# A two-layer decoder trunk in float32: W1 units between the seven-product pairs of the pass before

## The chip, the cores and the metric

The kernel runs on one core of a Trainium2 chip. The metric is the device time of one execution in microseconds; the figures are medians of several runs. TensorE is PE in the profile (its weight loads PEld), VectorE DVE, ScalarE ACT, GpSimd POOL, and SyncE, which here only issues transfers, SP.

## What is computed

The input is 256 positions of 2048 float32 values. Layer 0 is a gated short convolution and an MLP, layer 1 is attention (MLA) and an MLP; after each of the four sub-layers stands a layer norm of the scaled sum. The change lies in the two MLPs, which are the largest part: each multiplies 256 x 2048 by 2048 x 8192 and that by 8192 x 2048.

```python
def sq_relu_mlp(x, w1, w2):
    return jnp.square(jax.nn.relu(x @ w1)) @ w2

for layer in range(DEPTH):            # DEPTH = 2
    mix = short_conv_mixer(...) if layer < N_A else mla_mixer(...)
    h = layer_norm(ALPHA * h + mix, ln_g[layer, 0], ln_b[layer, 0])
    h = layer_norm(ALPHA * h + sq_relu_mlp(h, mlp_w1[layer], mlp_w2[layer]),
                   ln_g[layer, 1], ln_b[layer, 1])
return h
```

## The kernel before

**Split numbers.** Every float32 operand is held as two float32r parts: `hi`, a cast on ScalarE (line 127), and `lo`, the difference on VectorE (line 128). A product is then hi by hi, hi by lo and lo by hi, the sum taken in PSUM. The weights come raw from HBM, are split on the chip and used once.

**The stream of weights.** `stream` lists every weight tile in the order of use. `take(n, look)` hands over the next n and, before that, prepares what comes after them, up to `look` pieces ahead: a tile of W1 or a plain tile of W2 is one piece (one transfer of 512 KB, one `hi`, one `lo`), a pair for seven products is three (two transfers; `hi` and `lo` of three tiles of 1024 columns and one of 512, and the combinations that they are made of, lines 162 to 170). `RAW` tiles hold raw weights, `WA` pairs of tiles hold split ones. The transfers are issued on SP's queue.

**An MLP.** `mlp` goes over the 8192 hidden columns in `NQ` = 8 passes of 1024. A pass has `QC` = 8 units: unit m makes 128 hidden columns for all 256 positions, 32 matmuls on the 16 K tiles of W1 (`mm_run`: at each K tile `high`, 512 columns at line 215, and `low`, 256 columns at line 219). Its sums are put together by `whole` (ScalarE copies a half out of PSUM at line 355, VectorE adds the other at line 356), then relu and square (lines 718, 719) and the split. In the first unit of a pass, `TURNED` swaps `high` and `low` at one K tile.

After its eight units a pass multiplies the 1024 hidden columns by its part of W2. Passes 0 and 7 do it plainly. In the six passes between (`FAST`) two K tiles make a pair, and with two blocks of 128 positions and two blocks of 512 output columns a pair is a 2 x 2 product of blocks. `fast_products` computes that in seven products instead of eight (the Winograd form of Strassen's method; `FACTORS` names each product's two factors). The factors of the activations, the `forms`, are sums of blocks, made by `form` (lines 707 to 710) from two units. The output columns are two groups of 1024. In a pass, group 1 comes first, with three pairs of seven products and one plain pair of eight (`MIXED` = "sssp"; `EVEN` splits one of its matmuls in two), then group 0 with four pairs of seven. The products of three matmuls each are at lines 300, 302 and 303 (`dot`).

**The sums.** Each of the seven products has a PSUM bank and its own running sum over the passes: three in `acc`, four (`OWN`) in `sums`. Before a group starts, ScalarE copies running sums into PSUM (`resumed`, line 612); afterwards it copies them back (`put_back`, line 616), or VectorE adds what was begun from nothing (`keep`, line 624). In the last pass `fold` (line 676) combines the seven sums to four blocks. The residual of the layer norm waits in `xres` in SBUF meanwhile. In the first MLP `begin` (`ln.prepare`, line 415) scales it and takes a mean away before the layer's end; in the second, `extra` (`turn_residual`) turns it with TensorE and adds it to `acc` during passes 1 to 4.

**Order.** The program is written in one order; the instructions of each engine are put in order when the kernel is built, by the written order and by what is ready, and then run strictly in that order.

Of the kernel before, what the change touches and what calls it, by code (L numbers as in the profile page):

```python
# [16 lines left out]
P = 128  # L17
# [16 lines left out]
RAW, WA = 5, 8  # L34
# [3 lines left out]
MIXED = "sssp"  # L38
EVEN = (QC - 1, "22")
# [14 lines left out]
def trunk(ctx: ExitStack, tc: tile.TileContext, xT, vecs, lead, w_first, w_in, w_out, w_kv, w_q, w_uk, w_uv,  # L54
# [27 lines left out]

    def mlp_stream(l):
        out = []
        for q in range(NQ):
            out += halves(w1[l, q * QC:(q + 1) * QC])
            if q not in FAST:
                out += halves(w2[l, q])
                continue
            for j, kind in enumerate(MIXED):  # L90
                out += [(w2f[l, q, 1, j, 0], w2f[l, q, 1, j, 1])] if kind == "s" else \
                    halves(w2[l, q, 2, j]) + halves(w2[l, q, 3, j])
            out += [(w2f[l, q, 0, j, 0], w2f[l, q, 0, j, 1]) for j in range(QC // 2)]
        return out
# [210 lines left out]
    def held(x, t):  # L305

        return [x[:, o + t * P:o + (t + 1) * P] for o in (0, T)]
# [35 lines left out]
    def fast_products(ps, x, forms, j, fresh, ready, onto=()):  # L343

        b, = take(1)
        a = {"11": held(x[2 * j], 0), "12": held(x[2 * j + 1], 0), "22": held(x[2 * j + 1], 1)}
        for i in range(4):
            a[f"S{i + 1}"] = [forms[:, j, o, i * P:(i + 1) * P] for o in range(2)]
        for p, l, r in FACTORS:
            dot(ps[p], b[r], a[l], p in fresh, p in ready, onto=p in onto)  # L350
# [41 lines left out]
    class Norm:  # L392
# [10 lines left out]
        def prepare(self, m, bank=None):  # L403

            d = xres[:, m, :]
# [11 lines left out]
        def count(self, m):  # L417
            d = xres[:, m, :]
# [21 lines left out]
        def wide(self, m):  # L440
            d, x, g = xres[:, m, :], self.xd[m], self.gain(m)[0]
# [31 lines left out]
        def normal(self, m, dst=None):  # L473

            g, b = self.gain(m)
            d = xres[:, m, :]
# [22 lines left out]
    def add(ps, m):  # L499
        d = xres[:, m, :]  # L500
        nc.vector.tensor_tensor(d, d, ps[:, :T], ALU.add)
# [73 lines left out]
    def mlp(idx, ln, blocks, fast, begin=None, extra=None, last=False):  # L575
# [25 lines left out]
        sums = fast.tile([P, 4, 2, BW], F32, name=f"sums{idx}")  # L601

        def place(p, g):

            return sums[:, OWN.index(p), g, :] if p in OWN else \
                block(*{"2": (2 * g, 0), "3": (2 * g + 1, 0), "4": (2 * g, 1), "22": (2 * g + 1, 1)}[p])

        def resumed(p, g, name, bank):

            ps = psum(name, bank)  # L610
            if q != FAST[0] or p not in OWN:
                nc.scalar.copy(ps, place(p, g))
            return ps
# [4 lines left out]
        def keep(p, g, ps):  # L618

            at = place(p, g)  # L620
            if q == FAST[0] and p in OWN:
                nc.scalar.copy(at, ps)
            else:
                nc.vector.tensor_tensor(at, at, ps, ALU.add)

        def resume(busy, free, ps, m):

            b2, b3, b4, b6 = free
            b1, b5, b7, b22 = busy
            for p, bank in {3: (("3", b3),), 4: (("2", b2),), 5: (("4", b4), ("1", b1)), 6: (("6", b6), ("5", b5)),  # L630
                            7: (("7", b7), ("22", b22))}.get(m, ()):
                ps[p] = resumed(p, 1, f"ps_r{p}", bank)

        def down_pairs(h, forms, busy, free, ps):

            b2, b3, b4, b6 = free
            b1, b5, b7, b22 = busy
            new = set(OWN) if q == FAST[0] else set()
            onto = set(ps) - new
            for j, kind in enumerate(MIXED):  # L640
                if kind == "s":
                    last = j == MIXED.rindex("s")
# [545 lines left out]
```

## Time and profile before

| | |
|---|---|
| median of 3 runs | 2000.58 us (2000.33 to 2001.18) |
| span of the profiled execution, first to last instruction | 1994.9 us |
| that execution's own time | not recorded beside its span |
| first fast pass to the end of pass 7, first MLP | from 452.8 to 997.5 us |
| the same, second MLP | from 1394.6 to 1941.8 us |
| granted TensorE clock | 1.000 |
| moved by the DMA queues | 385.85 MB |

A row of the timeline is the start in us, the duration, the engine, the line, and out<-in by the program's names. Matmuls overlap, so what one costs is the time from its start to the next one's start, not its duration. The same holds, to a smaller degree, for VectorE and ScalarE. A row of a group is: line, engine, operation, out<-in, count, busy us, mean ns of one, idle time of the engine before them and what ended it. A row of the windows is: stretch and length in us, then the busy time of each engine with its number of instructions, the granted clock, the DMA engines' share and GB/s.

### The profile page before, as it was taken

To read this page: it belongs to the slowest core of one execution; us is meant where nothing else is said; L and a number is where in the kernel's file an instruction comes from. 1 tells how busy PE (TensorE), PEld (TensorE's weight loads), DVE (VectorE), ACT (ScalarE), POOL (GpSimd) and SP (SyncE) were. 2 spreads that over 40 slices of the span, in tenths; PEclk is the share of its full clock that TensorE was granted. 3 is DMA by queue.
4 is the path that set the end of the run, shared out by engine and by line. 5 is a ranking of instruction groups with operands and counts; after the bars stand their busy time and mean duration, and the time that the engine had idled before them with its cause. 6 is when DMAs were issued, how large, how long until landed. Compare 5 with 4: busy or idle time off the path is not lost.

```text
span 1994.9 us, 30180 instructions
## 1 busy us (share of the span) xinstructions
PE 1987.7 (100%) x11110; PEld 1737.2 (87%) x11110; DVE 1709.4 (86%) x2555; ACT 1354.9 (68%) x2154; POOL 2.3 (0%) x21
## 2 busy tenths in 40 slices
PE   9999999999999999999999999999999999999998
PEld 8888888988888888888889998898888888888886
DVE  8667667797999989989978988777899999999985
ACT  6444445586778778777756755558677787887772
POOL 0000000000000000000000000000000000000000
PEclk9999999999999999999999999999999999999999
DMA  8666666565657466574855543656464656656483
GB/s 318 205 191 187 190 190 190 179 193 157 212 170 251 148 216 221 177 243 147 281 171 159 170 140 123 201 180 195 146 233 155 232 161 220 222 178 233 150 269 130
DMA packets 106853, 385.85 MB, mean 193 GB/s; under 512 B 11857, under 2 KB 12625, under 8 KB 106449
## 3 DMA queue, kind: packets, MB, share of 16 engines
q1 hardware_dynamic: 106560, 383.79, 59.5%
q8 instruction: 87, 1.43, 0.3%
q14 instruction: 62, 0.50, 0.1%
q10 hardware_dynamic: 144, 0.13, 0.0%
HBM read 381.78 MB, written 2.10 MB: 192 GB/s over the span
## 4 chain that ended last, share of the span: by engine, by line
PE 98%; DVE 1%; ACT 1%; issue 0%; DVEq 0%; ACTq 0%
PE ps_u L215 20%; PE ps_l L215 13%; PE ps_u L219 10%; PE ps_l L219 7%; PE ps_f L300 4%; PE ps_f L303 4%; PE ps_f L302 4%; PE ps_r L303 4%; PE ps_r L302 4%; PE ps_r L300 4%; PE ps_d L300 2%; PE ps_d L302 2%; PE ps_d L303 2%; PE ps_w L249 2%; PE ps_w L248 2%; PE ps_w L247 2%
## 5 line engine op out<-in xcount | busy, mean ns | idle before, releaser
L128 DVE TENSOR_TENSOR lo<-raw,hi 128x1024 fp32r<-128x1024 f32 x710 | 861.8, 1220 | 190.6 <-ACT hi L127 119.9
L127 ACT CAST hi<-raw 128x1024 fp32r<-128x1024 f32 x710 | 741.8, 1051 | 247.4 <-PE ps_l L215 98.1
L215 PE MATMUL ps_u<-xhl,hi 128*128 128x512 f32 x1792 | 621.7, 392 | 0.0
L219 PE MATMUL ps_u<-xhl,lo 128*128 128x256 f32 x1792 | 498.2, 279 | 0.0
L215 PEld LDWEIGHTS ps_u<-xhl,hi 128*128 128x128 f32 x1792 | 334.5, 187 | 73.6 <-ACT acc L595 0.2
L219 PEld LDWEIGHTS ps_u<-xhl,lo 128*128 128x128 f32 x1792 | 338.1, 189 | 1.8
L215 PE MATMUL ps_l<-xhl_a,hi 128*128 128x512 f32 x704 | 244.1, 393 | 0.0
L219 PE MATMUL ps_l<-xhl_a,lo 128*128 128x256 f32 x704 | 195.4, 279 | 0.0
L215 PEld LDWEIGHTS ps_l<-xhl_a,hi 128*128 128x128 f32 x704 | 132.1, 188 | 29.9
L219 PEld LDWEIGHTS ps_l<-xhl_a,lo 128*128 128x128 f32 x704 | 131.9, 188 | 0.2
L127 ACT CAST hi_t<-raw_t 128x1024 fp32r<-128x1024 f32 x84 | 88.5, 1054 | 45.8 <-DVE raw_t L162 41.4
L162 DVE TENSOR_TENSOR raw_t<-raw,raw 128x1024 f32<-128x1024 f32 x84 | 102.3, 1218 | 1.8 <-DMA raw<-in_w2f_dram 1.5
L128 DVE TENSOR_TENSOR lo_t<-raw_t,hi_t 128x1024 fp32r<-128x1024 f32 x84 | 102.4, 1219 | 0.2
L718 ACT ACTIVATE fp<-fp 128x256 f32<-128x256 f32 x96 | 40.0, 416 | 63.2 <-DVE fp L356 62.6
L215 PE MATMUL ps_l<-z,hi 128*128 128x512 f32 x240 | 82.4, 391 | 0.0
L300 PE MATMUL ps_d<-hi,h 128*128 128x512 f32 x192 | 75.0, 391 | 0.0
L302 PE MATMUL ps_d<-lo,h 128*128 128x512 f32 x192 | 75.0, 390 | 0.0
L303 PE MATMUL ps_d<-hi,h 128*128 128x512 f32 x192 | 74.8, 389 | 0.0
L249 PE MATMUL ps_w<-xd,hi 128*128 128x258 f32 x256 | 72.7, 284 | 0.0
L248 PE MATMUL ps_w<-xd,lo 128*128 128x258 f32 x256 | 72.3, 282 | 0.0
L247 PE MATMUL ps_w<-xd,hi 128*128 128x258 f32 x256 | 72.3, 282 | 0.0
L215 PE MATMUL ps_l<-oT,hi 128*128 128x512 f32 x208 | 71.3, 391 | 0.0
(296 smaller groups left out, 3963.7 us busy)
## 6 DMA issues: line engine op xcount, KB each, us to landing
raw<-in_w_dram SPq DMA_DIRECT2D x344, 512.0 KB, 4.5
raw<-in_w2f_dram SPq DMA_DIRECT2D x168, 512.0 KB, 3.9
raw<-in_w_in_dram SPq DMA_DIRECT2D x88, 512.0 KB, 4.2
raw<-in_w_out_dram SPq DMA_DIRECT2D x32, 512.0 KB, 3.7
raw<-in_w_o_dram SPq DMA_DIRECT2D x32, 512.0 KB, 4.2
raw<-in_w_kv_dram SPq DMA_DIRECT2D x10, 512.0 KB, 3.7
raw<-in_w_q_dram SPq DMA_DIRECT2D x8, 512.0 KB, 4.0
raw<-in_w_uk_dram SPq DMA_DIRECT2D x8, 512.0 KB, 3.9
```

Of the source, the lines that this page charges most:

```text
L127: nc.scalar.copy(hi, src)
L128: nc.vector.tensor_tensor(lo, src, hi.bitcast(F32), ALU.subtract)
L162: nc.vector.tensor_tensor(t.rearrange(two, a=2), b12.unsqueeze(1).to_broadcast([P, 2, BW]), r1.rearrange(two, a=2), ALU.subtract)
L215: nc.tensor.matmul(ps, w[blk // 8][0][:, blk % 8, :], x, start=first, stop=False)
L219: nc.tensor.matmul(ps[:, :T], w[blk // 8][1][:, blk % 8, :], x[:, :T], start=False, stop=last)
L247: nc.tensor.matmul(ps[:, :W], hi, x[k][:, :W], start=k == 0, stop=False)
L248: nc.tensor.matmul(ps[:, :W], lo, x[k][:, :W], start=False, stop=False)
L249: nc.tensor.matmul(ps[:, :W], hi, x[k][:, W:], start=False, stop=k == NC - 1)
L300: nc.tensor.matmul(ps, x[0], w[0], start=first, stop=False, skip_group_check=onto)
L302: nc.tensor.matmul(ps[:, at], x[0], w[1][:, at], start=False, stop=False, skip_group_check=onto)
L303: nc.tensor.matmul(ps, x[1], w[0], start=False, stop=last, skip_group_check=onto)
L718: nc.scalar.activation(f, f, AF.Relu)
```

## The change

Group by group and pass by pass becomes step by step. A step is one W1 unit of the running pass, followed by one pair of seven products that belongs to units made `SHIFT` = 5 steps and more before: pass 1's units 0 to 4 have no pair beside them, then 48 steps have one, and pass 7's units 5 to 7 have none. All 48 pairs of an MLP use seven products.

- The groups alternate like a snake (pass 1: group 1, then 0; pass 2: 0, then 1), so that a group goes on from one pass into the next. Once in each pass, after the fourth pair, all seven banks are copied out and the other group's seven copied in (`put_back` and `resume`, both ScalarE). `keep` is gone.
- The seven sums and a unit take the eight banks: all units of paired steps use the bank "unit"; units without a pair take turns on "6" and "unit".
- A pair's relu, square, forms and split are made at once over both units in one tile `u` of 8 x 128 columns; the seven left factors lie side by side in `factors` and are split in one go of 7 x 128 columns.
- Every unit that follows a pair has the turned step (`TURN`).
- The ring grows (`RAW` 5 to 7, `WA` 8 to 9), and `take` prepares 7 pieces ahead at a unit and 6 at a pair. `sums` takes the place of the residual in SBUF: in the first MLP the residual is prepared in pass 1, sent to DRAM by five transfers and fetched back by four of 512 KB after pass 7, on GpSimd's queue; in the second, `extra` reads it in the first four units of pass 1.

```diff
-RAW, WA = 5, 8
+RAW, WA = 7, 9
-MIXED = "sssp"
-EVEN = (QC - 1, "22")
+SHIFT = 5
+
+
+def TURN(q, m):
+    return m == 0 or not (q == 1 and m < SHIFT or q == NQ - 1 and m > SHIFT)
...
+    held_x = [xres]
+    parked = ctx.enter_context(tc.tile_pool(name="parked", bufs=1, space=bass.MemoryType.DRAM)).tile(
+        [P, NC, T], F32, tag="parked", name="parked")
...
+    def steps():
+
+        for q in range(1, NQ):
+            for m in range(QC):
+                p, i = (q, m - SHIFT) if m >= SHIFT else (q - 1, m + QC - SHIFT)
+                yield q, m, (p, i // NB, i % NB, (p % 2) ^ (i // NB)) if p in FAST else None
...
+    LEFT = ("11", "22", "12", "S1", "S3", "S2", "S4")
+
+    def fast_products(ps, x, j, fresh, ready, onto=()):
+
+        b, = take(1, 6)
+        a = {n: [x[j // 2][:, j % 2, o, i * P:(i + 1) * P] for o in range(2)] for i, n in enumerate(LEFT)}
         for p, l, r in FACTORS:
             dot(ps[p], b[r], a[l], p in fresh, p in ready, onto=p in onto)
...
+        def form(u):
+
+            a21, a11, a12, s1, s2, s4 = (u[:, i * P:(i + 1) * P] for i in (0, 1, 3, 4, 6, 7))
+            two = u.rearrange("p (i c) -> p i c", c=P)
+            nc.vector.tensor_tensor(s1, a21, u[:, 2 * P:3 * P], ALU.add)
+            nc.vector.tensor_tensor(two[:, 5:7, :], two[:, 0:5:4, :], a11.unsqueeze(1).to_broadcast([P, 2, P]),
+                                    ALU.subtract)
+            nc.vector.tensor_tensor(s4, a12, s2, ALU.subtract)
+
+        def finish_pair(j, u):
+            f = factors[j // 2][:, j % 2]
+            if q in FAST:
+                form(u)
+                split(f[:, 0, :], f[:, 1, :], u[:, P:])
+            else:
+                split(f[:, 0, :2 * T], f[:, 1, :2 * T], u[:, :2 * T])
...
+        base = Banks.count
+        bank = {p: (base + i) % 8 for i, p in enumerate(("6", "unit", "3", "1", "5", "7", "2", "4"))}
+        factors = [act.tile([P, QC // 4, 2, 7 * P], F32R, tag=tag, name=f"h{idx}{tag}") for tag in ("c", "a2")]
...
+        def resume(p, g, at=None):
+
+            ps[p] = psum(f"ps_{p}", bank[at or p])
+            onto.discard(p)
+            if p in OWN and begun[g] == FAST[0]:
+                fresh.add(p)
+            else:
+                nc.scalar.copy(ps[p], place(p, g))
+                onto.add(p)
...
+        def products_of(p, i, j, g):
+
+            nonlocal folds
+            order = [f[0] for f in FACTORS]
+            end = i == 0 or p == FAST[-1]
+            fast_products(ps, factors, j, set(fresh), order if j == NB - 1 and end else (), onto)
+            fresh.clear()
+            if j == NB - 1 and end:
+                begun[g] = 0
+                for o in order:
+                    put_back(o, g, ps[o])
+                    if i == 0:
+                        resume(o, 1 - g)
+            if p == FAST[-1] and j == NB - 1:
+                folds = chain(folds, fold(g))
+
+        for q, m, pair in steps():
+            lone = pair is None
+            if q == FAST[0] and m == SHIFT:
+                for o, _, _ in FACTORS:
+                    resume(o, 1)
+            w = take(2, 7)
+            at = "6" if lone and m % 2 == 0 else "unit"
+            un = psum("ps_u", bank[at])
+            mm_run([(w, un)], xhl, 0, NC, NC, turned=TURNED if TURN(q, m) else None)
+            if m % 2 == 0:
+                u = fast.tile([P, 8 * P], F32, tag="fp", name="fp")
+            whole(un, u[:, (m % 2) * T:(m % 2 + 1) * T])
+            if m % 2:
+                for function in (AF.Relu, AF.Square):
+                    nc.scalar.activation(u[:, :2 * T], u[:, :2 * T], function)
+                if m > 1 or lone:
+                    finish_pair(m // 2, u)
+            if extra and q == FAST[0] and m < NB:
+                for t in range(2):
+                    extra(block, m, t, spare[1 + (2 * m + t) % 3])
+            if begin and q == FAST[0] and m < SHIFT:
+                begin(range(3 * m + 1, 3 * m + 4))
+                nc.gpsimd.dma_start(parked[:, 3 * m + (m > 0):3 * m + 4, :], held_x[0][:, 3 * m + (m > 0):3 * m + 4, :])
+            if q == FAST[0] and m == SHIFT:
+                sums = act.tile([P, 4, 2, BW], F32, tag="xres", name=f"sums{idx}")
+            if q == NQ - 1:
+                for _ in range(3 if m >= SHIFT else 2):
+                    next(folds, None)
+            if pair:
+                products_of(*pair)
+            if m == 1 and not lone:
+                finish_pair(0, u)
...
+        held_x[0] = act.tile([P, NC, T], F32, tag="xres", name="xback")
+        for k in range(0, NC, 4):
+            nc.gpsimd.dma_start(held_x[0][:, k:k + 4, :], parked[:, k:k + 4, :])
+        Banks.count = base + 2
+        blocks(block, put, h)
```

More of the change, by code (lines that the diff above doesn't have):

```diff
@@ L440, in wide @@
         def wide(self, m):
[L441 removed]
+            d, x, g = held_x[0][:, m, :], self.xd[m], self.gain(m)[0]
             nc.scalar.activation(x[:, :T], d, AF.Copy, scale=g)
@@ L615, in put_back @@
         def put_back(p, g, ps):
             nc.scalar.copy(place(p, g), ps)
[L618 to L632, printed above, removed]
@@ L760, in mlp @@
[L760 to L774 removed]
+                    ln.finish()
@@ new lines, in mlp @@
+                ps = ws[m][1]
+            else:
+                ws = [(take(), psum("ps_w"))]
+                mm_wide(ws, ln.xd)
+                ps = ws[0][1]
+            f = tmp.tile([P, T], F32, tag="fh", name="fh", bufs=3)
+            ln.weighted(ps, f, AF.Relu)
+            nc.scalar.activation(f, f, AF.Square)
+            put_split(h[m], f)
+        acc = act.tile([P, 2, D], F32, tag="a1", name=f"acc{idx}")
+        for n in range(NB):
+            down(h, put, n)
+            if begin and n == 1:
+                begin(range(1), (Banks.count + 4) % 8)
```

194 lines of the change are left out of this document (46 added, 148 removed).

## The prediction

> **What bounds the kernel now.** I read the page first (the span, the busy table, the slices, the chain that ended last), then TensorE's waits.
>
> ```profile
> span 1994.9 us, 30180 instructions
> PE 1987.7 (100%) x11110; PEld 1737.2 (87%) x11110; DVE 1709.4 (86%) x2555; ACT 1354.9 (68%) x2154; POOL 2.3 (0%) x21
> DVE  8667667797999989989978988777899999999985
> PE 98%; DVE 1%; ACT 1%; issue 0%; DVEq 0%; ACTq 0%
> ...
> PE ps_e L1075 <- ACT umeans L1073: 1.6, 1, 1.6
> PE warm L372 <- DVE col L373: 1.0, 1, 1.0
> PE ps_f L300 <- ACT acc L616: 0.5, 1, 0.5
> ```
>
> The chain is 98% TensorE, and TensorE waits three times in the whole execution, 3.1 us together. Time can therefore be saved only by giving TensorE less to stream, and it can be lost wherever a new wait reaches it. VectorE is the engine that is nearly full: its slices stand at 8 and 9 in the middle passes. The granted clock is 1.000 throughout, so a matmul has one price.
>
> That price comes from the start times in TensorE's timeline. `ps_u` rows begin a W1 unit, the `ps_r` and `ps_f` rows begin the products of column groups 1 and 0.
>
> ```profile
> 702.46 0.39 PE L215 MATMUL ps_u<-xhl,hi 128*128 128x512 f32 x1
> 708.02 0.39 PE L215 MATMUL ps_u<-xhl,hi 128*128 128x512 f32 x1
> 746.85 0.39 PE L300 MATMUL ps_r<-hi,forms 128*128 128x512 f32 x1
> 748.93 0.39 PE L300 MATMUL ps_r<-hi_t,forms 128*128 128x512 f32 x1
> 766.64 0.39 PE L300 MATMUL ps_f<-hi,forms 128*128 128x512 f32 x1
> 785.68 0.39 PE L215 MATMUL ps_u<-xhl,hi 128*128 128x512 f32 x1
> 868.91 0.39 PE L215 MATMUL ps_u<-xhl,hi 128*128 128x512 f32 x1
> 953.06 0.39 PE L215 MATMUL ps_u<-xhl,hi 128*128 128x512 f32 x1
> ```
>
> One fast pass is 785.68 - 702.46 = 83.22 us: eight units in 44.39, group 1 in 19.79, group 0 in 19.04. Group 0 is four pairs of seven products, so one such pair is 4.76 us (84 matmuls at 0.2267). The first unit, the one with the turned step, is 5.56 us, the other seven (746.85 - 708.02) / 7 = 5.547. The first nine matmuls after the units take 748.93 - 746.85 = 2.08 us against 9 x 0.2267 = 2.04, so going from a unit to products costs 0.04. The last fast pass of this layer is 953.06 - 868.91 = 84.15 us, 0.93 more than the others, and holds the third of the waits above.
>
> **What the interleaving saves TensorE.** Group 1 is now three fast pairs and one plain pair of eight products: 19.79 - 3 x 4.76 - 0.04 = 5.47 us for the plain pair (25 matmuls, one of them split in two). It becomes a fast pair, 4.76: 0.71 us less in each of the twelve passes (six in each layer). Interleaving gives part of it back. There are eight ways from a unit into products instead of one (7 x 0.04 = 0.28), and eight turned units instead of one (7 x 0.013 = 0.09). A step is then 5.56 + 0.04 + 4.76 = 10.36 us, a pass 82.9, and the gain 0.32 us x 12 = 3.8 us. The eight units without a pair in each layer (five in pass 1, three in pass 7) cost what they cost now. Why the turned step is needed at every head shows where a unit runs without it:
>
> ```profile
> 273.06 0.40 PE L215 MATMUL ps_u<-z,hi 128*128 128x512 f32 x1
> 278.71 1.08 PE L215 MATMUL ps_l<-z,hi 128*128 128x512 f32 x4
> ```
>
> That unit, the same 32 matmuls, took 5.65 us, 0.10 more than 5.547.
>
> **What it does to VectorE.** The windows split the same pass into its units and its products, and the timeline gives start-to-start costs.
>
> ```profile
> core 0: us, PE busy (x) PEld busy (x) DVE busy (x) ACT busy (x) POOL busy (x), PEclk, DMA share, GB/s
> 702.50:746.90 44.40, 44.40 (x258) 39.13 (x257) 39.47 (x57) 34.20 (x56) 0.00 (x0) 1.00 0.61 210
> 746.90:785.70 38.80, 38.80 (x174) 32.11 (x174) 38.63 (x45) 31.20 (x47) 0.00 (x0) 1.00 0.57 181
> 702.50:785.70 83.20, 83.20 (x430) 71.25 (x429) 78.10 (x101) 65.40 (x102) 0.00 (x0) 1.00 0.59 197
> ...
> 713.57 0.39 PE L215 MATMUL ps_u<-xhl,hi 128*128 128x512 f32 x1
> ...
> 713.80 0.28 DVE L708 TENSOR_TENSOR sf<-fp 128x128 f32<-128x128 f32 x1
> 714.00 1.22 DVE L128 TENSOR_TENSOR lo<-raw,hi 128x1024 fp32r<-128x1024 f32 x1
> 717.05 0.42 DVE L356 TENSOR_TENSOR fp<-ps_u,t 128x256 f32<-128x256 f32 x1
> 717.42 1.23 DVE L128 TENSOR_TENSOR lo<-raw,hi 128x1024 fp32r<-128x1024 f32 x1
> 718.56 0.28 DVE L707 TENSOR_TENSOR sf<-fp 128x128 f32<-128x128 f32 x1
> 720.55 0.69 DVE L128 TENSOR_TENSOR h<-fp,h 128x512 fp32r<-128x512 f32 x1
> 721.15 0.69 DVE L128 TENSOR_TENSOR forms<-sf,forms 128x512 fp32r<-128x512 f32 x1
> ```
>
> In the products VectorE has no gap left (38.63 of 38.80); in the units it has 4.9 us. Back to back, 1024 columns cost 1.14 us (717.42 to 718.56), 512 cost 0.60 (720.55 to 721.15), 128 cost 0.20 (713.80 to 714.00). A fast pair's weights are four operations of 1024 (three low parts and `raw_t`) and three of 512: 6.36 us, more than the 4.76 that TensorE spends on them. A plain pair's are two low parts, 2.28. So per pass VectorE gains 4.08. It loses the three `keep` additions of 512 (1.80), and the forms shrink: four of 128 and two of 512 (2.0 us) become 128, 256 and 128, and a low part of 896 (about 1.75 on the line through the rows), four times, 1.0. Net: 78.1 + 1.3 = 79.4 us of work in a pass of 82.9, 96%. Today the same engine swings between 89% and 100%; in the interleaved order each step of 10.36 us brings about 9.9 of it, evenly. I take this at nothing: the slack is small, 3.5 us a pass, but seven pieces (half a unit or a third of a pair) are now prepared ahead of a unit where it was five. If that cover is gone, TensorE waits for the difference. ScalarE is further off (65.40 of 83.2) and loses ten of 24 PSUM copies.
>
> **What else moves.** The `begin` subtractions are written into the last pass today, yet ran before the first unit:
>
> ```profile
> 434.57 0.42 DVE L415 SCALAR_TENSOR_TENSOR xres<-xres,mu 128x256 f32<-128x256 f32 x1
> ```
>
> so their place in the program matters little; in pass 1 they meet units without products, where a step of 5.55 us holds some 4.5 of VectorE. The eight `turn_residual` calls of layer 3 keep their transposes. `fold` goes from 8 operations of 1024 (9.1 us) to 16 of 512 (9.6), still in pass 7. The residual goes out by five transfers and comes back by four of 512 KB, all on POOL's queue, where nothing else of these passes waits; they are priced with their rival.
>
> **The new waits.** First, all units of paired steps share one PSUM bank, so a unit waits until the evacuation before it is done. That has the pair's 0.04 + 4.76 = 4.80 us. In the rows above the unit before ended at 713.57 and its evacuation at 717.05 + 0.42 = 717.47, 3.90 us later: covered, with 0.9 over. In the worst pass it isn't:
>
> ```profile
> 891.12 0.39 PE L215 MATMUL ps_u<-xhl,hi 128*128 128x512 f32 x1
> ...
> 895.93 0.42 DVE L356 TENSOR_TENSOR fp<-ps_u,t 128x256 f32<-128x256 f32 x1
> 902.80 0.68 DVE L128 TENSOR_TENSOR forms<-sf,forms 128x512 fp32r<-128x512 f32 x1
> ```
>
> That is 896.35 - 891.12 = 5.23 us. Second, the fourth pair of a pass is finished after unit 7 and multiplied one step later: its evacuation, relu, square, forms and split have 4.80 + 5.56 = 10.36 us. Today the same chain ends 721.15 + 0.69 - 713.57 = 8.27 us after its unit, and in the worst pass 903.48 - 891.12 = 12.36. The worst pass is late because its VectorE fell behind in the products of the passes before, which the even load takes away, so I take both at nothing.
>
> Third, the crossing: in the middle of each pass seven banks are copied out and seven in, on ScalarE, while TensorE finishes the pair and does one unit.
>
> ```profile
> L616 ACT COPY sums<-ps_r x48: 572/587/604, 508.3 to 1874.9; 128x512 f32<-128x512 f32 x48
> L612 ACT COPY ps_r<-sums x40: 572/579/585, 543.1 to 1856.9; 128x512 f32<-128x512 f32 x40
> ```
>
> Fourteen at 0.58 are 8.1 us against 4.08 us of the remaining products and 5.56 of the unit, 9.6 us: covered, but ScalarE's casts stand behind them, and VectorE's low parts behind the casts. Today's crossings cost 0 in a pass of 83.22 and 0.93 in the last of layer 1; those are the ends, and nearest to the first, I take 0.2 for each of twelve, 2.4 us (0 to 11.2).
>
> **The sum.** -3.8 (products) - 0.9 (the wait of today's last pass, which the even load removes) + 2.4 (crossings) = -2.3 us. The profiled span of 1994.9 us becomes 1992.6; the page records no time of that execution beside its span, and the median of the runs, 2000.58, lies 5.7 us above it, which I leave as it is: 1998.3 us. A difference under 0.2%, 4.0 us, is about what a measurement of this kernel can tell from none, so this counts as the same.
>
> **The rivals.**
>
> *No wait at all.* The crossings are free, as in the pass of 83.22: -4.7 us, 1995.9. For it: the load is evened out and the ring is deeper. Against it: 96% of VectorE leaves 3.5 us a pass. Chance 0.24.
>
> *The fourth pair comes late (the other side).* Place: the first products of a pass's second step after unit 7. It decides as soon as the chain from unit 7 takes over 10.36 us. It is one operation longer in ScalarE's part (relu and square over 512 columns), and VectorE, at 96%, makes each of its hops wait behind a low part of 1.14. At the worst row's 12.36 us in every pass TensorE waits 2.0 x 12 = 24 us, 2022; in half of them 12 us, 2010. The bank of the units, at 5.23 against 4.80, would add to the same lateness. For it: today's rows of 8.27 and 12.36 straddle the limit. Chance 0.25.
>
> *Half the units fall out of step.* A pair has 21 matmuls, an odd count, where today's passes hold 172 between units. If the turned step sets the pace for one parity alone, 48 of the 96 paired units pay 0.10: +4.9, 2003.2. For it: today `EVEN` splits one matmul, which makes the count even. Chance 0.05.
>
> *The residual comes back late.* Layer 1's tail adds to it from 1020.3 on:
>
> ```profile
> L501 DVE TENSOR_TENSOR xres<-xres,turned x16: 412/415/422, 1020.3 to 1060.7; 128x256 f32<-128x256 f32 x16
> raw<-in_w_dram SPq DMA_DIRECT2D x344, 512.0 KB, 4.5
> ```
>
> The sums leave its place when pass 7 ends (about 997.5 today), so the first transfer has 22.8 us and the fourth some 60, 15 each. SP's transfers of that size land in 4.5 us. It decides when POOL's take over 15 us; at 20 each the last is 20 us late, 2018. Before has no transfer on POOL, so no row prices one. Chance 0.04. [...]
>
> **How the numbers follow.** The forecast, 1996.6 to about 2004, has 0.42; no wait 0.24; the late pair 0.25; the units out of step 0.05; the residual 0.04. Faster by over 0.2% (below 1996.6) is the second alone, 0.24; slower (above 2004.6) is the late pair and the residual, 0.29; the rest, 0.47, is within. The range runs from 1995.5, which takes in the case without waits, to 2012, which takes in the late pair in half the passes; the other half of that rival and the residual, some 0.17, lie above. The likeliest case's own range is 1996.6 to 2004.
>
> **What would show it.** Right: a fast pass near 82.9 us between the same units of two passes; four matmuls fewer in each pass (168 instead of 172 beside the units) and no plain pair; TensorE's waits still a few, at `ps_u` or at the first products after a crossing; VectorE at 95 to 97% in every step, without the swing. Wrong: TensorE waiting in most steps for the evacuation or for the forms' low part (the late pair); units of 5.65 us behind every second pair (out of step); waits in layer 1's tail that end with a POOL transfer (the residual). If TensorE waits longest for weights' low parts all through a pass, VectorE has become the bound, and the whole argument from the even load is wrong.

## The result, and the profile after

The changed kernel takes 2007.56 us (median of 5 runs, 2006.16 to 2009.80); the kernel before, run beside it, 2000.47 us (5 runs, 1997.57 to 2001.18). The ratio is 1.0042, 95% interval 1.003 to 1.0055: slower by 0.4%, where no change was forecast. The forecast was 1998.3; the time lies inside the range given with it, in the part that the range had taken in for the rival "the fourth pair comes late". The profiled execution took 2009.8 us, the longest of the five, with a span of 2007.7.

The page of the changed kernel (its span and busy table), and TensorE's waits:

```profile
span 2007.7 us, 29769 instructions
PE 1990.3 (99%) x11062; PEld 1733.5 (86%) x11062; DVE 1719.5 (86%) x2493; ACT 1291.6 (64%) x1914; POOL 7.3 (0%) x30
```

```profile
PE ps L309 <- ACT h1a L136: 3.4, 4, 1.1
PE ps L309 <- ACT h3a L136: 3.2, 3, 1.1
PE ps L312 <- DVE h3a L137: 2.1, 1, 2.1
PE ps L312 <- DVE h1a L137: 1.9, 1, 1.9
PE ps_e L1064 <- ACT umeans L1062: 1.6, 1, 1.6
PE warm L383 <- DVE col L384: 1.1, 1, 1.1
```

The last two waits were there before. The first four rows are new, and all of one kind: a product (L309, L312) waits for `h1a` or `h3a`, which hold the factors of pairs 2 and 3 (counted from 0; pair 3 is the fourth). The digit is the sub-layer: 1 is the first MLP and 3 the second, and so are the prediction's "layer 1" and "layer 3". No wait for a unit's evacuation (`ps_u`) is in the list, and the one that before had in the last fast pass of its first MLP is gone.

TensorE's timeline shows where they lie. Each row below is the first matmul of a W1 unit: unit 7 of pass 3, unit 7 of pass 4, unit 0 of pass 5, unit 1 of pass 5.

```profile
671.63 0.39 PE L224 MATMUL ps_u<-xhl,hi 128*128 128x512 f32 x1
754.56 0.39 PE L224 MATMUL ps_u<-xhl,hi 128*128 128x512 f32 x1
764.93 0.39 PE L224 MATMUL ps_u<-xhl,hi 128*128 128x512 f32 x1
776.52 0.39 PE L224 MATMUL ps_u<-xhl,hi 128*128 128x512 f32 x1
```

The first two are a pass apart: 82.93 us, as computed (82.9). The next step takes 10.37, also as computed. The step of unit 0, which ends in the fourth pair's product, takes 11.59: 1.22 too many. Each MLP has four such steps, behind passes 1, 4, 5 and 6. Against 10.37, the excess is 4.24, 1.22, 1.35 and 1.39 us in the first MLP, and 3.96, 1.22, 1.35 and 1.33 in the second: 16.1 us, four times the 3.8 us of the product saving. The four rows of waits make up 10.6 of it, and two stretches at half the clock, shown below, about 3.2; the other 2.3 were not taken apart.

The chain of the fourth pair around such a step, in the timelines of TensorE, ScalarE and VectorE:

```profile
760.12 0.39 PE L309 MATMUL ps<-hi,h1a 128*128 128x512 f32 x1
...
760.94 0.36 ACT L366 COPY t<-ps_u 128x256 f32<-128x256 f32 x1
...
763.62 0.63 ACT L730 ACTIVATE fp<-fp 128x512 f32<-128x512 f32 x1
764.15 1.05 ACT L136 CAST hi<-raw 128x1024 fp32r<-128x1024 f32 x1
765.09 0.64 ACT L730 ACTIVATE fp<-fp 128x512 f32<-128x512 f32 x1
...
770.67 0.93 ACT L136 CAST h1a<-fp 128x896 fp32r<-128x896 f32 x1
...
762.40 0.42 DVE L367 TENSOR_TENSOR fp<-ps_u,t 128x256 f32<-128x256 f32 x1
762.73 1.21 DVE L137 TENSOR_TENSOR lo<-raw,hi 128x1024 fp32r<-128x1024 f32 x1
763.87 0.68 DVE L137 TENSOR_TENSOR t<-raw,t 128x512 fp32r<-128x512 f32 x1
764.47 2.35 DVE L137 TENSOR_TENSOR lo<-raw,hi 128x1024 fp32r<-128x1024 f32 x2
766.74 0.28 DVE L645 TENSOR_TENSOR fp<-fp 128x128 f32<-128x128 f32 x1
766.94 1.22 DVE L137 TENSOR_TENSOR lo<-raw,hi 128x1024 fp32r<-128x1024 f32 x1
768.08 0.42 DVE L646 TENSOR_TENSOR fp<-fp 128x256 f32<-128x256 f32 x1
768.41 1.22 DVE L171 TENSOR_TENSOR raw_t<-raw,raw 128x1024 f32<-128x1024 f32 x1
769.55 0.28 DVE L648 TENSOR_TENSOR fp<-fp 128x128 f32<-128x128 f32 x1
...
771.65 0.50 PE L309 MATMUL ps<-hi,h1a 128*128 128x512 f32 x1 [1.00 <-ACT h1a L136]
```

Unit 7 of pass 4 ends at 760.12, where the first row has the next product begin. Its factors' high part is ready at 770.67 + 0.93 = 771.60, 11.48 us later; the step gives 10.37. The chain's own operations are short. Between its evacuation (L367) and its last form (L648) VectorE does four low parts of 1024 columns, one of 512 and a `raw_t`, 6.3 us of weights' preparation in the chain's 7.4. Relu and square (L730) stand behind casts in the same way. The same order comes behind unit 7 of passes 5 and 6, and three times in the second MLP. Behind passes 2 and 3 the high part is ready 9.1 and 10.0 us after unit 7, and TensorE doesn't wait.

The windows of this step, of the one ahead of it and of the one behind it show VectorE's load (after the length: PE, PEld, DVE, ACT, POOL busy):

```profile
754.56:764.93 10.37, 10.37 (x55) 8.83 (x53) 10.30 (x13) 6.61 (x9) 0.00 (x0) 1.00 0.55 203
764.93:776.52 11.59, 10.59 (x54) 8.82 (x53) 11.55 (x16) 8.54 (x14) 0.00 (x0) 1.00 0.60 197
776.52:786.89 10.37, 10.37 (x55) 8.84 (x53) 6.66 (x7) 10.37 (x18) 0.00 (x0) 1.00 0.53 186
```

VectorE is busy for 10.30 us of the first step, but for 6.66 of the step behind the crossing, in which ScalarE does most of the fourteen copies and is busy throughout. So a pass holds about the work that was forecast (78.25 us in the 82.93 from 702.73 on, forecast 79.4), but not evenly: most of the slack lies in the one step behind the crossing, and at unit 7 there is none.

The larger waits, at the end of the first interleaved pass (one in each MLP), add two things. First TensorE's and VectorE's timelines, then the windows (busy times of the engines, granted clock, DMA share, GB/s):

```profile
520.45 0.50 PE L312 MATMUL ps<-hi,h1a 128*128 128x512 f32 x1 [1.87 <-DVE h1a L137]
...
521.85 0.63 PE L309 MATMUL ps<-hi_t,h1a 128*128 128x512 f32 x1
522.27 0.63 PE L311 MATMUL ps<-lo_t,h1a 128*128 128x512 f32 x1
...
518.17 1.23 DVE L171 TENSOR_TENSOR raw_t<-raw,raw 128x1024 f32<-128x1024 f32 x1 [0.80 <-DMA raw<-in_w2f_dram]
519.31 1.08 DVE L137 TENSOR_TENSOR h1a<-fp,h1a 128x896 fp32r<-128x896 f32 x1
```

```profile
521.10:524.40 3.30, 3.30 (x9) 2.54 (x8) 2.50 (x4) 2.14 (x4) 0.00 (x0) 0.50 0.49 155
```

VectorE's queue holds a `raw_t` that waits 0.80 us for its transfer, and the fourth pair's low part stands behind it. The window that begins 0.65 us after the wait of 1.87 us has a granted clock of 0.50 for its 3.3 us, and a matmul takes 0.42 to 0.43 us where it takes 0.2267 otherwise: eight of them, another 1.6 us.

### The profile page after: what moved, and what is told of

It is laid out like the page before. It is cut to its first block, busy times and chain, and to the rows that moved or that the text cites. A ratio compares the mean times of both kernels' runs of the same rounds, so it can differ in the third digit from the quotient of the medians.

```text
span 2007.7 us, 29769 instructions
## 1 busy us (share of the span) xinstructions
PE 1990.3 (99%) x11062; PEld 1733.5 (86%) x11062; DVE 1719.5 (86%) x2493; ACT 1291.6 (64%) x1914; POOL 7.3 (0%) x30
## 4 chain that ended last, share of the span: by engine, by line
PE 87%; DVE 8%; issue 3%; DMA 1%; ACT 1%; DVEq 0%; ACTq 0%
PE ps_u L224 16%; PE ps_l L224 13%; PE ps_u L228 8%; PE ps_l L228 7%; PE ps L312 6%; PE ps L309 6%; PE ps L311 6%; DVE lo L137 3%; PE ps_d L309 2%; PE ps_d L312 2%; PE ps_d L311 2%; PE ps_w L258 2%; PE ps_w L257 2%; PE ps_w L256 2%; DVE raw_t L171 1%
## 5 line engine op out<-in xcount | busy, mean ns | idle before, releaser
L137 DVE TENSOR_TENSOR lo<-raw,hi 128x1024 fp32r<-128x1024 f32 x710 | 855.3, 1218 | 175.8 <-ACT hi L136 105.7
L228 PE MATMUL ps_u<-xhl,lo 128*128 128x256 f32 x1792 | 485.4, 280 | 0.0
L136 ACT CAST hi_t<-raw_t 128x1024 fp32r<-128x1024 f32 x96 | 101.5, 1058 | 133.5 <-DVE raw_t L171 126.1
L171 DVE TENSOR_TENSOR raw_t<-raw,raw 128x1024 f32<-128x1024 f32 x96 | 116.8, 1217 | 10.6 <-DMA raw<-in_w2f_dram 10.6
L137 DVE TENSOR_TENSOR lo_t<-raw_t,hi_t 128x1024 fp32r<-128x1024 f32 x96 | 116.9, 1218 | 1.1 <-ACT hi_t L136 1.0
L366 ACT COPY t<-ps_u 128x256 f32<-128x256 f32 x112 | 41.5, 371 | 89.7 <-PE ps_u L228 89.5
L730 ACT ACTIVATE fp<-fp 128x512 f32<-128x512 f32 x112 | 71.5, 638 | 8.8 <-DVE fp L367 8.1
L178 DVE TENSOR_TENSOR raw<-raw 128x512 f32<-128x512 f32 x96 | 66.2, 690 | 2.4
L175 DVE TENSOR_TENSOR raw<-raw,raw_t 128x512 f32<-128x512 f32 x96 | 65.7, 684 | 1.0
```

Of the source, the lines that this page charges most:

```text
L136: nc.scalar.copy(hi, src)
L137: nc.vector.tensor_tensor(lo, src, hi.bitcast(F32), ALU.subtract)
L171: nc.vector.tensor_tensor(t.rearrange(two, a=2), b12.unsqueeze(1).to_broadcast([P, 2, BW]), r1.rearrange(two, a=2), ALU.subtract)
L228: nc.tensor.matmul(ps[:, :T], w[blk // 8][1][:, blk % 8, :], x[:, :T], start=False, stop=last)
L730: nc.scalar.activation(u[:, :2 * T], u[:, :2 * T], function)
```

## The experiments

Theory A: VectorE is at its limit in a pass (with the time it stands starved at each crossing), and the fourth pair is where it shows first. Theory B: VectorE has enough time, but unit 7's chain stands behind weights' preparation in the queues, and only the fourth pair has a consumer one step behind. The starved time is the 3.7 us in which VectorE is idle in the step from 776.52 above.

All times below are medians beside runs of the kernel before on the same chip (1998.3 to 1999.6 us); the ratio is to those. Those medians differ by up to 1.3 us from chip to chip, so times of runs on different chips can differ by as much without an edit. The edits also change the order in which the engines' work is written out: VectorE's order is the same as in the changed kernel up to 523 us with the copies left out or moved to VectorE, up to 840 us with the third pair's factors, and up to 52 us with one piece fewer ahead.

**The crossings' copies left out.**

```
-                    put_back(o, g, ps[o])
+                    if p == FAST[-1]:
+                        put_back(o, g, ps[o])
...
-            if p in OWN and begun[g] == FAST[0]:
+            if begun[g] == 0 or p in OWN:
                 fresh.add(p)
```

> The crossings' copies of the middle passes are left out (the sums of the passes before are not carried, so most of the down products' sum is missing); nothing else changes. Theory A (the crossing starves VectorE): in the changed kernel VectorE stands idle 3.7 us in the step of each crossing, with 79.9 us of work in a pass of 82.9, so it runs at its limit through the pass and the fourth pair's chain comes late. Without the copies that idle time goes, the chain from unit 7 ends before 10.3 us after it in every pass, and the six waits of about 1.2 us go: 2007.6 - 7.3 = 2000.3 us, the two larger waits at the end of the first interleaved pass (4.2 us each) staying. Theory B (the chain of unit 7 is too long by its own hops, whatever the crossing does): the waits of 1.2 us stay, 2006 to 2008 us.

2053.16 us, ratio 1.0271 (1.0257 to 1.0285): neither. VectorE now waits for transfers all through the passes (71.3 us against 10.6 in the changed kernel, in the waits of VectorE):

```profile
DVE raw_t L171 <- DMA raw<-in_w2f_dram: 71.3, 57, 3.2
```

Taking the copies out changed the order of VectorE's queue from the first crossing on. So the run doesn't isolate the crossing. That the new order is what makes the transfers late is likely, but not shown.

**The third pair's factors twice.**

```
-            fast_products(ps, factors, j, set(fresh), ...
+            fast_products(ps, factors, 2 if i == 0 and j == NB - 1 else j, set(fresh), ...
```

> The first column group's fourth product takes the third pair's factors a second time in place of the fourth pair's, so TensorE doesn't wait for the chain of unit 7 there (that product is a wrong one; the fourth pair is still finished, and used four steps later). Theory B (only that chain is late): all eight waits go and nothing takes their place: 2007.6 - 16.1 = 1991.5 us. Theory A (VectorE is at its limit, 79.9 us of work and 3.7 to 4.2 us of starved time in a pass of 82.9): the lateness of 0.7 to 1.2 us a pass goes on growing through passes 4 to 7 and meets TensorE elsewhere, at the units' evacuation or the weights' low parts: 1994 to 2000 us.

1994.91 us, ratio 0.9979 (0.997 to 0.9988). TensorE's waits:

```profile
PE ps_e L1064 <- ACT umeans L1062: 1.6, 1, 1.6
PE warm L383 <- DVE col L384: 1.1, 1, 1.1
PE ps_u L224 <- DVE fp L367: 0.6, 2, 0.4
```

The eight waits are gone, and besides the two that were there before only two of 0.6 us together are in the list. Up to 840 us VectorE's order is that of the changed kernel, so there only the consumer has been taken away: behind pass 4 the chain is as late as before (11.5 us), and TensorE goes on without a wait. In the next two passes, where the order differs, the chain takes 8.1 and 8.6 us: the lateness does not go on growing, as theory A expected it to. The time lies in theory A's range and 3.4 us above the 1991.5 of theory B; but the 16.1 us were read in the execution of 2009.8 us and taken off the median. Off that execution they give 1993.7, 1.2 under this run.

**Each copy out made twice** (`put_back` a second time for all passes but the last).

> Each of the seven copies out of a crossing is made twice (the last pass's are not): 7 x 0.58 = 4.1 us more of ScalarE's time in each of ten crossings, the same results. Theory A: ScalarE's casts come 4.1 us later, VectorE's starved time grows from 3.7 to 7.8 us, and as it has no slack left each pass gets longer by about that: +41 us, 2040 to 2050 us. Theory B (ScalarE is busy for two thirds of the time and the crossing is covered): 2008 to 2012 us.

2017.18 us, ratio 1.0096 (1.0082 to 1.011): 9.6 us above the changed kernel for 41 us more of ScalarE's work. The waits are now at weights' casts after the crossing, in six passes of ten:

```profile
PE ps L309 <- ACT hi L136: 10.6, 6, 1.8
```

So the crossing has room, though not 4.1 us of it (if the changed order plays no part): theory B's "covered" was too good, theory A's "no slack" far off.

**Three of the seven copies out on VectorE.**

```
+            if p in ("1", "7", "6"):
+                nc.vector.tensor_copy(place(p, g), ps)
+            else:
+                nc.scalar.copy(place(p, g), ps)
```

> Three of the seven copies out of a crossing move from ScalarE to VectorE, into the time in which it is starved: 3 x 0.6 = 1.8 us more work for VectorE, 1.7 us less for ScalarE, whose casts come that much sooner. Theory A: the starved 3.7 us shrink by about 3.5 (the three copies and the earlier casts), VectorE gains 1.7 us net in a pass, more than the 1.2 it is late: the six waits go, about 2000.3 us, or less if the two larger ones shrink as well. Theory B (VectorE's work alone sets the chain): 1.8 us more of it a pass make the waits longer, 2008 to 2018 us.

2001.11 us, ratio 1.0012 (1.0003 to 1.0021). The six excesses of 1.2 to 1.4 us are gone, as theory A had it; of the two larger ones, one stays (4.6 us) and the other falls to 1.3. Behind every pass from 2 to 6 the high part is now ready after 9.1 us. This fits that the starved time makes VectorE later at unit 7; the order of the queue has changed as well, and the run doesn't part the two.

**One step more of room** (`SHIFT = 6`, a second buffer for `u`, pairs 0 and 1 finished after the products that free their factors, `RAW = 6`).

> Every product comes one step later behind its pair (SHIFT 6), so the chain of unit 7 has two steps, 20.7 us, in place of 10.3; the units' tile gets a second buffer, which one buffer of the weight ring pays for (RAW 6). Theory B (only the chain of unit 7 is late, and nothing else waits): all eight waits go, 16.1 us: 2007.6 - 16.1 = 1991.5; the run with the third pair's factors, where TensorE met no wait either, had 1994.9, so 1991 to 1996 us. Theory A (VectorE as such is too slow by 0.7 to 1.2 us a pass): the lateness is met at the weights' low parts or the evacuation instead, 1997 to 2005 us. A shorter ring that matters: over 2005 us.

1995.88 us, ratio 0.999 (0.9981 to 0.9999). All eight waits are gone, also with the shorter ring; two others of 0.7 us together are left. This is what theory B expected.

**Relu and square by unit.**

```
-                for function in (AF.Relu, AF.Square):
-                    nc.scalar.activation(u[:, :2 * T], u[:, :2 * T], function)
...
+            for function in (AF.Relu, AF.Square):
+                nc.scalar.activation(u[:, (m % 2) * T:(m % 2 + 1) * T], ..., function)
```

> Relu and square run on each unit's 256 columns right after its evacuation in place of both units' 512 after the second: the same results, two more ScalarE operations a pair, the chain of unit 7 shorter by some 2 x 0.25 us and perhaps by one place in VectorE's queue (1.14). Theory B in the form that the chain's own hops make it late: the six waits of 1.2 us shrink to 0.1 to 0.7 each: 2001 to 2005 us. In the form that VectorE's 2.2 us of lateness at unit 7 (0.5 at the others) makes it late: hardly a change, 2006 to 2008 us.

2002.51 us, ratio 1.0022 (1.0013 to 1.0031). The six smaller excesses are gone altogether; of the two larger ones, one stays (4.4 us) and the other falls to 2.4.

**The ring as it was.** `RAW, WA = 5, 8`, `take(2, 5)`, `take(1, 5)`.

> The weight ring as it was before the change (5 raw tiles, 8 parts, five pieces ahead), all else as in the changed kernel: what the deeper ring brings. If seven pieces carry VectorE over the 3.7 us of the crossing, five don't: waits for weights in every crossing on top, 2012 to 2030 us. If the depth doesn't matter, and the chain of unit 7 alone does: 2005 to 2010 us.

2014.91 us, ratio 1.0084 (1.007 to 1.0098): slower, as expected, but not by the waits for weights that were expected. TensorE waits for evacuations (7.3 us, ten times) and once in each MLP for 3 us or more for the fourth pair. Raw tiles, parts and pieces ahead are all fewer here, so the run doesn't say which of them counts.

**Two of a fast pair's subtractions on GpSimd** (L175 and L178: `nc.vector` becomes `nc.gpsimd`).

> The two subtractions of 512 columns in each fast pair's weights (0.6 and 0.7 us) move from VectorE to GpSimd, which does nothing in these passes: 1.3 us less for VectorE in each step of 10.36. If VectorE's lateness at unit 7 is what makes the chain late, VectorE now has 13 us of slack a pass, is early everywhere, and all waits go: 1991 to 1996 us. [...]

2113.38 us, ratio 1.0581 (1.0566 to 1.0595). Groups of POOL and VectorE in that run (count, busy us, mean ns, then idle time):

```profile
L178 POOL TENSOR_TENSOR raw<-raw 128x512 f32<-128x512 f32 x96 | 189.7, 1976 | 177.5 <-issue 128.5 <-DVE lo L137 28.8 <-DMA raw<-in_w2f_dram 15.5
L175 POOL TENSOR_TENSOR raw<-raw,raw_t 128x512 f32<-128x512 f32 x96 | 139.8, 1457 | 1037.0 <-DVE raw_t L171 833.9 <-DMA raw<-in_w_dram 203.1
L137 DVE TENSOR_TENSOR lo_t<-raw_t,hi_t 128x1024 fp32r<-128x1024 f32 x96 | 144.7, 1507 | 52.0 <-ACT hi_t L136 51.9
L648 DVE TENSOR_TENSOR fp<-fp 128x128 f32<-128x128 f32 x48 | 23.5, 489 | 0.4
```

In the changed kernel the two on VectorE take 684 and 690 ns, `lo_t` 1218 and the form of L648 283. GpSimd's 1457 and 1976 ns are 2.1 and 2.9 times as long. In the passes of this run, VectorE's low part of 1024 columns takes 1.22 us when no subtraction runs on GpSimd and 2.01 on average beside one, the form of L648 0.28 and 0.64, and L367, one of whose inputs lies in PSUM, 0.41 and 0.42.

**Fewer pieces ahead, more raw tiles.** `RAW, WA = 9, 8`, `take(2, 6)`, `take(1, 5)`.

> The ring with nine raw tiles in place of seven, and eight parts in place of nine (six and five pieces looked ahead, not seven and six). In the changed kernel's larger wait, at the end of the first interleaved pass, VectorE's queue holds a weight's subtraction that waits 0.8 to 1.0 us for its transfer, ahead of the fourth pair's low part. If the transfer is late because its raw tile comes free late, nine tiles let it start earlier and the two waits of 4.2 us shrink by half or more: 2001 to 2004 us. If one look-ahead piece less counts for more (the old ring of 5 and 8 had 2014.9): 2007 to 2013 us.

1995.38 us, ratio 0.998 (0.9971 to 0.9989). Better than either expectation: of the new waits one of 0.8 us is left. The six smaller ones are gone as well, which no theory had tied to the ring.

**A shorter chain.** Relu and square by unit, `S3` made after unit 6, and the forms after unit 7:

```
-            nc.vector.tensor_tensor(s1, a21, u[:, 2 * P:3 * P], ALU.add)
-            nc.vector.tensor_tensor(two[:, 5:7, :], two[:, 0:5:4, :], a11..., ALU.subtract)
+            nc.vector.tensor_tensor(two[:, 4:7:2, :], two[:, 0:6:5, :], a22..., ALU.add)
             nc.vector.tensor_tensor(s4, a12, s2, ALU.subtract)
```

> The chain of unit 7 made shorter without moving it: relu and square by unit, S3 = A21 - A11 made from unit 6 alone, S1 and S2 in one operation of 256 columns from A22, then S4: two VectorE operations after unit 7 in place of three, the rest of the changed kernel as it is. Theory B (only that chain is late): its end moves about 2 us ahead of the 11.4 us it took, or 1.1 ahead of relu and square by unit (8.3); the six waits of 1.2 us go, and the larger two shrink from 4.2 to 1 to 3 us: 1995 to 2000 us. If the larger two hang on a weight's transfer ahead in VectorE's queue, they stay as they were with relu and square by unit: 2001 to 2003 us.

1997.18 us, ratio 0.9989 (0.998 to 0.9998). All but 1.2 us of the eight waits is gone; one of 0.5 us for an evacuation has come.

**The short chain and the three copies together.**

> The short chain and the three copies on VectorE together. Theory B: the six waits are gone with either, so nothing is added: the same as the short chain alone, within 1 us. Theory A (VectorE's lateness counts elsewhere too): 1 to 3 us better than the short chain alone.

1996.29 us, ratio 0.9987 (0.9978 to 0.9996): 0.9 us less than the short chain alone. The eleven times of one hardly overlap with those of the other (1995.79 to 1996.92 against 1996.50 to 1998.04, on the same chip), so this is a gain, though a small one: within theory B's 1 us and below what theory A expected.

**The short chain and one step more of room.**

> One step later (SHIFT 6, RAW 6) and the short chain together. With two steps of room no wait of the fourth pair was left (0.7 us in all at other places), so the shorter chain has nothing to gain there: 1995 to 1997 us, as one step later alone (1995.9). A gain of 1 us or more would show that evacuation and forms still delay TensorE somewhere.

1996.97 us, ratio 0.9988 (0.9979 to 0.9997): nothing gained on 1995.88 (ratio 0.999), as expected.

**One piece fewer ahead, the same raw tiles.** `RAW, WA = 7, 8`, `take(2, 6)`, `take(1, 5)`.

> Six and five pieces looked ahead and eight parts, as in the run with nine raw tiles, but the changed kernel's seven raw tiles. If one piece less ahead of the chain in VectorE's queue took the waits away: 1995 to 1998 us here too. If the two raw tiles did it, the transfers come late again and the waits are back: 2003 to 2013 us (between the changed kernel's 2007.6 and the old ring's 2014.9 on the slow side).

1994.85 us, ratio 0.9982 (0.9973 to 0.9991). The two more raw tiles are not needed. Pieces ahead and parts were lowered together and not taken apart. TensorE's waits, then the chain of the fourth pair in the same place as above (the first product behind unit 7, ScalarE, VectorE):

```profile
PE ps_e L1064 <- ACT umeans L1062: 1.6, 1, 1.6
PE warm L383 <- DVE col L384: 1.1, 1, 1.1
```

```profile
757.10 0.39 PE L309 MATMUL ps<-hi,h1a 128*128 128x512 f32 x1
...
758.16 1.30 ACT L730 ACTIVATE fp<-fp 128x512 f32<-128x512 f32 x2 [0.49 <-DVE fp L367]
...
762.73 0.93 ACT L136 CAST h1a<-fp 128x896 fp32r<-128x896 f32 x1
...
757.71 0.42 DVE L367 TENSOR_TENSOR fp<-ps_u,t 128x256 f32<-128x256 f32 x1 [0.30 <-ACT t L366]
758.05 1.22 DVE L171 TENSOR_TENSOR raw_t<-raw,raw 128x1024 f32<-128x1024 f32 x1
759.30 0.69 DVE L175 TENSOR_TENSOR raw<-raw,raw_t 128x512 f32<-128x512 f32 x1
759.91 0.28 DVE L645 TENSOR_TENSOR fp<-fp 128x128 f32<-128x128 f32 x1
760.11 0.68 DVE L178 TENSOR_TENSOR raw<-raw 128x512 f32<-128x512 f32 x1
760.71 0.42 DVE L646 TENSOR_TENSOR fp<-fp 128x256 f32<-128x256 f32 x1
761.05 1.22 DVE L137 TENSOR_TENSOR lo_t<-raw_t,hi_t 128x1024 fp32r<-128x1024 f32 x1
762.18 0.28 DVE L648 TENSOR_TENSOR fp<-fp 128x128 f32<-128x128 f32 x1
```

VectorE stands idle 0.30 us before the evacuation, so no preparation delays it. Relu and square run back to back in place of behind two casts. Between L367 and L648 there are two operations of 1024 columns and two of 512, not five and one. The high part is ready at 762.73 + 0.93 = 763.66, 6.56 us after the unit's end, where it took 11.48. A pass has the same pieces; with one fewer allowed ahead they come at another time.

Read in the same way behind unit 7 of each pass of the first MLP, the high part is ready after (us):

| pass | 1 | 2 | 3 | 4 | 5 | 6 |
|---|---|---|---|---|---|---|
| changed kernel | 10.7 | 9.1 | 10.0 | 11.5 | 11.6 | 11.6 |
| one piece fewer ahead | 10.1 | 9.6 | 7.8 | 6.6 | 6.6 | 6.6 |

So the edit doesn't shorten every chain. It does so from pass 3 on, and behind pass 1, where the larger wait was for the low part, that part is ready after 11.2 us instead of 13.3.

**Nine raw tiles and the short chain.**

> Nine raw tiles, eight parts, and the short chain. Only one wait of 0.8 us was left to take away, and the first operation of each chain adds work to VectorE (one operation more a pair, 0.2 us): 1994.5 to 1996 us, the same as nine raw tiles alone (1995.4). More than 1 us less would show a loss that the waits don't.

1993.52 us (8 runs, 1993.19 to 1993.93), ratio 0.9974 (0.9964 to 0.9984): the best of all, 5.2 us under the kernel before on the same chip (1998.76), and 1.9 under nine raw tiles alone, more than expected. Its TensorE has only the two waits that all versions have. This doesn't show a loss beyond the waits: of the 2.0 us between the two profiled spans (1993.2 and 1991.2), 0.9 is there at 50 us already, where VectorE's order is the same in both, and the rest arises in the first MLP, where nine raw tiles alone has its wait of 0.8.

**Nine raw tiles and the three copies.**

> Nine raw tiles, eight parts, and three of the seven copies out of a crossing on VectorE. If the crossing's starved time (still 2.7 to 4.7 us with nine tiles) costs nothing once the chain is early: 1994.5 to 1996 us. If it costs, 1 to 3 us less.

1997.14 us, ratio 0.999 (0.9981 to 1.0): 1.8 us worse than nine raw tiles alone, which neither expectation had. Small waits for the fourth pair are back: behind passes 4 to 6 its high part is ready after 10.7 us, where it took 6.6. The edit that took six waits out of the changed kernel brings six small ones into this one, so its worth probably lies in what it does to the order of the queues; this was not tested by itself.

## Why the prediction was wrong

*The products: right.* 82.93 us for a pass against 82.9, 10.37 for a step against 10.36, and 48 matmuls fewer (11062 against 11110). (The 84 matmuls that the prediction names beside 4.76 us are those of four pairs; one pair has 21.) With the new waits gone the time is 3.9 us under before (one piece fewer ahead) to 5.2 (the best run); the sum without waits gave 4.7 (the rival "no wait at all").

*The turned step at both parities: right.* Units take 5.57 us in every step; "half the units out of step" did not come.

*The residual: right.* POOL's four transfers of 512 KB back took 8.1 us (median), not the 4.5 of SP's, but under the 15 from which they would count; no wait behind the first MLP ends with one.

*The units' single bank: right.* No wait for an evacuation in the changed kernel.

*The crossings: the term 2.4 us.* No wait of TensorE ends with one of the copies. But VectorE stands starved for 3.7 to 4.1 us behind the crossings of passes 2 to 5. The prediction named the casts and low parts behind the copies and then asked only whether TensorE would wait.

*The wait in the last fast pass of the first MLP: went, as said.*

*The fourth pair: the step that failed.* "The worst pass is late because its VectorE fell behind in the products of the passes before, which the even load takes away, so I take both at nothing." The rows of 8.27 and 12.36 us lay on both sides of the limit of 10.36, and the longer was explained away by load. Two things were wrong in this. First, the load did not become even: each step was to bring about 9.9 us of VectorE's work, and the sign for being right was 95 to 97% in every step. Measured are some 10.3 of 10.37 in most steps and 6.7 in the one behind the crossing, so that at unit 7 VectorE has nothing to spare, though the total over a pass was right. Second, what the chain has to pass was left out. In the changed kernel 6.3 us of weights' preparation stand between its hops on VectorE, and the high part is ready after 11.5 us where the step gives 10.37. The prediction had the reason in hand: "are now prepared ahead of a unit where it was five" was counted as cover alone. That the late fourth pair is the loss is shown by the third pair's factors and by one step more of room, which both take all eight waits away. Why it is late is shown in part: one piece fewer ahead, a shorter chain, and less starved time each take away the six smaller waits, and each also changes the order of the queues, so depth, load and order were not parted.

The rival had the place and the mechanism. Its price of 2.0 us a pass was 1.2 to 1.4 in six passes, about 4 in two and nothing in four: 16.1 us, between its half (12) and its whole (24). The two of about 4 hold a term that it didn't have, the stretch at half the clock (1.6 us each).

*The time outside the span* was taken as 5.7 us. It was 2.1 in the profiled execution of the changed kernel (2009.8 against 2007.7) and 1.7 to 1.9 in every later execution of the kernel before, whose times go from 1996.0 to 2002.9 us. So the page of before was that of a quick execution, of about 1997 us. The difference that was forecast, -2.3 us, doesn't hang on it.

## What to carry to other kernels

A look-ahead is not cover alone: on engines that work through a fixed order, what is prepared ahead can stand in front of a late result that must pass the same queue (here 6.3 us of it in a chain's 7.4). Where a chain has a consumer one step behind, count the queue ahead of each of its hops at the moment that it starts, not the engine's share of busy time over a whole pass: 78 us of 83 seemed to leave room, and the room did not lie where the chain ran. When one such chain is late, one piece fewer ahead is a cheap thing to try: here it changed three numbers (one of them the parts) and did as much as a shorter chain or a whole step of room (a ratio of 0.9982 against 0.9989 and 0.999). It is no rule: the old ring, with two fewer and fewer raw tiles, was slower (1.0084 against the changed kernel's 1.0042).

## What the runs showed of the hardware

Two waits of TensorE in the changed kernel, of 1.87 us and, in the second MLP, of 2.07, were followed within 1.5 us by 3.3 us at a granted clock of 0.50 (the first in the window above, the second from 1473.40 to 1476.70); after the six waits of 1.0 to 1.1 us the matmuls kept their 0.2267 us. In the run with each copy out made twice TensorE waited six times for a weight's cast, 10.6 us together and 1.8 at most, and the mean granted clock of that execution was 0.999. Six such stretches would have made it 0.995, an estimate (6 x 3.3 us at half the clock in the span of 2015.2 us). So waits only a little shorter were mostly not followed by such a stretch; what decides it is not shown.

In the run with two subtractions on GpSimd, its subtraction of 512 columns took 1457 (L175) and 1976 ns (L178) on average, against VectorE's 684 and 690 in the changed kernel. VectorE's `lo_t` took 1507 ns on average over that run against 1218, the form of L648 489 against 283, and the sum of L367, with one input in PSUM, 413 against 417. Beside a running subtraction the low parts of 1024 columns took 1.65 times as long as without one (2.01 us against 1.22) and the form of L648 2.3 times (0.64 against 0.28); L367 took 0.42 against 0.41. Why they differ so is not shown.
